# Differential attention of a two-layer trunk: the loads of the next head's queries and keys written in the order of need, and the gates ended at 600 units of attention instead of 640

## The chip, the core and the metric

The kernel runs on one core of one Trainium2 chip. The metric is the device time of one execution in microseconds (us), from the first to the last instruction with the little that lies around them. Lower is better.

## The reference, cut to what matters

Two layers work on 2048 tokens of width 1024. Layer 0 is a windowed attention beside a chunked one, with gates and an output projection; the change leaves it alone. Layer 1 is differential attention with 8 heads: each head has two queries and two keys of 64 columns, and one value of 128 columns.

```
q, k, v, gate = split(h @ w_in)
mask = key chunk <= query chunk                 # chunks of 64 tokens
p1 = softmax(where(mask, q1 @ k1.T / 8, -1e30))
p2 = softmax(where(mask, q2 @ k2.T / 8, -1e30))
o  = (p1 - lam * p2) @ v
o  = rms_norm(o, subln_g) * (1 - lambda_init)
y  = x + (o * silu(gate)) @ w_out
```

All is float32. The kernel keeps each operand as two float32r parts, a high one (H) and a low one (L), and takes a product as two or three matmuls.

## The kernel before, in words

The 2048 tokens are 4 blocks of 512. Layer 1 first projects all tokens (lines named p1) and stores queries, keys and values in DRAM. Then one long stage runs attention, gates and output projection together. It is this stage that the change touches.

**Heads.** The blocks of queries go from 3 down to 0, and in each the 8 heads in order. I write 3.5 for block 3, head 5. A head of block b needs b+1 key tiles for each of its two halves (k0 and k1, with z the number of the key block, so k0z2 is block 2 of the first key) and b+1 value tile pairs. `scores` goes over 4 rows of 128 queries (j); for each it goes over the half m, and for each half over the key blocks z: two matmuls (L867, L868) into a PSUM bank, a maximum on VectorE (L871), an exponential on ScalarE (L874). Then GpSimd scales and combines the two probability rows (L895 to L901). `values` transposes the probabilities (L914), splits them (L917, L918) and multiplies by the values (L921 to L923).

**Side work.** Between these steps stand matmuls that need no attention: `gates` (tiles cG, 288 steps, the eighth chunk of columns of each block of tokens also reloading the 16 tiles of hidden state p1hH, p1hL that the next block of tokens needs), then the output projection of the blocks 3, 2 and 1 (tiles com, 72 steps each), then that of block 0. After the last gates the same 16 tiles take the output weights (wo1H, wo1L). A table, `STAGES1`, says how many side steps shall be done after so many units of attention: a unit is a piece of 128 queries by 128 keys of a head, its scores (both halves) and its values counted half each. A head has 58 units in block 3, 42 in block 2, 26 in block 1 and 10 in block 0, so block 3 ends at 464 units and block 2 at 800.

**Buffers.** A key tile has 4 buffers for each half, as many as one head of block 3 uses. The key tiles of the next head can only be loaded when the last row (j = 3) of the present head has read the old ones, in the order k0z0, k0z1, k0z2, k0z3, k1z0 and on. Queries have 2 buffers, value tiles 4 for each part, gate weights 3 for each part.

**Order.** All transfers are issued by SP, one queue in a fixed order, and an SP row that has to wait holds all rows behind it. Each key tile takes two rows, one for kH and one for kL (L977, L978), queries four for each of qd and ql (L848, L849), values one for each part (L984), gate weights one for each part (L1007). The order on each engine isn't the order of the source: when the program is built, a scheduler places each instruction by its own estimate of when it is ready, and among the ready ones that come first in the source come first. In the source a head began with all its loads: for each key block the keys k0 and k1 and then the value pair (`load`), then the queries inside `scores`.

Of the kernel before, what the change touches and what calls it, by code (L numbers as in the profile page):

```python
# [18 lines left out]
P = 128  # L19
# [12 lines left out]
def f32(ap):  # L32
    return ap.bitcast(F32)
# [52 lines left out]
class Trunk:  # L86
# [727 lines left out]
    def _mix1(self, es):  # L814
# [22 lines left out]

        count = [0]

        def scores(h, b, K, res):  # L840

            tok = slice(b * BLK, (b + 1) * BLK)
            qd = qp.tile([P, 2, BLK], F32R, tag="qd", name=n + "qd")
            ql = qp.tile([P, 2, BLK], F32R, tag="ql", name=n + "ql")
            for m in range(2):
                r = slice(m * HD, (m + 1) * HD)
                for part, q in (("qH", qd), ("qL", ql)):
                    nc.sync.dma_start(f32(q[0:HD, m, :]), s[part][h, r, tok])  # L848
                    nc.sync.dma_start(f32(q[HD:P, m, :]), s[part][h, r, tok])  # L849
            us = res["u"] = []  # L850
            for j in range(NTB):
                t = b * NTB + j
                nk = (t + 1) * P
                cuts = [(c, min(nk, c + 512)) for c in range(0, nk, 512)]
                nb = len(cuts)
                js = slice(j * P, (j + 1) * P)
                nm, la, e = small("nm", 8), small("la", 8), small("e", 8)
                nm, la, e = (x.rearrange("p (m z) -> p m z", m=2) for x in (nm, la, e))
                l, rl = small("l", 2), small("rl", 2)
                rows = []  # L860
                for m in range(2):
                    chunks = []
                    for z, (c, ce) in enumerate(cuts):
                        wd = ce - c
                        ps = pS.tile([P, 512], F32, tag="S", name=n + "S")[:, :wd]
                        kt = K[z][m]
                        mm(ps, qd[:, m, js], kt[:, :wd], start=True, stop=False)  # L867
# [6 lines left out]
                        nc.scalar.activation(chunks[z][:, :wd], ps, AF.Exp, bias=nm[:, m, z:z + 1], accum_out=acc)  # L874
                        yield wd / 256
                    rows.append(chunks)
                if nb > 1:
                    top, pe = small("top", 2), small("pe", 8).rearrange("p (m z) -> p m z", m=2)[:, :, :nb]
                    nc.vector.tensor_reduce(top, nm[:, :, :nb], AX.X, ALU.min)
                    for m in range(2):  # L880
                        nc.scalar.activation(e[:, m, :nb], nm[:, m, :nb], AF.Exp, bias=top[:, m:m + 1], scale=-1.0)
                    nc.vector.tensor_tensor(pe, e[:, :, :nb], la[:, :, :nb], ALU.mult)
                    nc.vector.tensor_reduce(l, pe, AX.X, ALU.add)
                nc.vector.reciprocal(rl, l)  # L884
                cs = small("cs", 8).rearrange("p (m z) -> p m z", m=2)
                if nb > 1:
# [17 lines left out]
        def values(h, b, V, res):  # L904
            us = res["u"]
            O = pO.tile([P, BLK], F32, tag="O", name=n + "O")
            nkt = (b + 1) * NTB
            for kt in range(nkt):
# [8 lines left out]
                nc.scalar.activation(H[:, :wd], tp[:, :wd], AF.Copy)  # L917
                nc.vector.tensor_tensor(L[:, :wd], tp[:, :wd], f32(H[:, :wd]), ALU.subtract)  # L918
                o = O[:, j0 * P:]
                vH, vL = (v[:, kk:kk + P] for v in V[kt // 4])  # L920
                mm(o, vH, H[:, :wd], start=(kt == 0), stop=False, skip_group_check=True)  # L921
                mm(o, vH, L[:, :wd], start=False, stop=False, skip_group_check=True)  # L922
                mm(o, vL, H[:, :wd], start=False, stop=(kt == nkt - 1), skip_group_check=True)  # L923
# [43 lines left out]
            pl, tag = homes[b].pop(0)  # L967
            return pl.tile([P, BLK], F32R, tag=tag, name=n + "y" + tag)

        def load(h, i, K, V):  # L970

            tok = slice(i * BLK, (i + 1) * BLK)
            ks = []
            for m in range(2):
                k = kp.tile([P, BLK], F32R, tag=f"k{m}", name=n + f"k{m}")
                r, o = slice(m * HD, (m + 1) * HD), slice((1 - m) * HD, (2 - m) * HD)
                nc.sync.dma_start(f32(k[r, :]), s["kH"][h, r, tok])  # L977
                nc.sync.dma_start(f32(k[o, :]), s["kL"][h, r, tok])  # L978
                ks.append(k)
            K.append(ks)  # L980
            vs = []
            for part in ("vH", "vL"):
                v = vp.tile([P, BLK], F32R, tag=part, name=n + part)
                nc.sync.dma_start(  # L984
                    f32(v).rearrange("p (t c) -> p t c", t=NTB), s[part][tok, h * P:(h + 1) * P].rearrange("(t p) c -> p t c", p=P)
                )
                vs.append(v)
            V.append(vs)

        room = self.last_hidden  # L990

# [89 lines left out]
        at = [NB - 1]  # L1081

        def heads():
            for b in reversed(range(NB)):
                at[0] = b
                for h in range(8):
                    K, V = [], []
                    for i in range(b + 1):
                        load(h, i, K, V)
                    res = {}  # L1090
                    yield from scores(h, b, K, res)
                    queue.append(values(h, b, V, res))
            queue.append(leave())

        def leave():
# [59 lines left out]
```

## Time and profile before

| | |
|---|---|
| median of 3 runs | 2971.23 us (2970.77 to 2974.16) |
| the profiled execution | 2984.29 us |
| its span, first to last instruction | 2982.5 us |
| mean granted TensorE clock | 0.966 |
| TensorE matmuls busy | 2731.6 us, 92% of the span |
| VectorE, ScalarE, GpSimd busy | 65%, 53%, 54% |
| attention stage of layer 1 | from 1842.7 us to the end |

The profiled execution is 13 us above the median, so a sum made against the one is carried to the other by its ratio. The attention stage is read by stretches between the starts of heads; a start is the first of a head's own L867 matmuls, which are 32 for a head of block 3, 24 in block 2, 16 in block 1 and 8 in block 0, counted in order of time. In these stretches "PEclk" is the granted share of the TensorE clock.

### The profile page before, as it was taken

Reading aid. Unit: us, or ns where it says so; the run is one execution under the profiler, and the core shown is the slowest. Engines: PE = TensorE matmul, PEld = TensorE weight load, DVE = VectorE, ACT = ScalarE, POOL = GpSimd, SP = SyncE. Lnnn points to the kernel's source line nnn. Section 1 sums busy time; section 2 is a strip of 40 time slices with the busy share of each in tenths; the row PEclk is TensorE's granted clock in tenths of the full one; section 3 lists DMA queues with packets and bytes.
Section 4 is the critical chain, followed back from the end, with each engine's and each line's share of the span. In section 5 each row is a group of like instructions: output and inputs, shape, how many; then the busy total and the mean of one; then the engine's idle time right before and its main releaser. Section 6 shows DMA issues by size and latency. Waiting matters only on the chain.

```text
span 2982.5 us, 45078 instructions
## 1 busy us (share of the span) xinstructions
PE 2731.6 (92%) x13672; PEld 2260.0 (76%) x13672; DVE 1927.5 (65%) x4652; ACT 1589.7 (53%) x4135; POOL 1597.2 (54%) x1966
## 2 busy tenths in 40 slices
PE   7999999987888889999999997989989989998889
PEld 5888888876777778777788886767777767776667
DVE  7762475156777775598728852656667876887762
ACT  4443543366666565343344321656667765777661
POOL 3542252145344343267645740767777876888761
PEclk9999999999999999999999999989999999999999
DMA  4673344569988885567884455675767647657683
GB/s 152 224 250 123 103 149 127 185 189 254 258 228 209 221 212 150 185 224 236 264 295 160 127 184 164 192 202 166 217 179 219 193 127 233 170 163 203 164 256 120
DMA packets 422929, 572.40 MB, mean 192 GB/s; under 512 B 47648, under 2 KB 198176, under 8 KB 422688
## 3 DMA queue, kind: packets, MB, share of 16 engines
q1 hardware_dynamic: 422688, 569.53, 65.6%
q8 instruction: 109, 1.79, 0.3%
q14 instruction: 132, 1.08, 0.1%
HBM read 408.95 MB, written 160.43 MB: 191 GB/s over the span
## 4 chain that ended last, share of the span: by engine, by line
PE 66%; DMA 13%; DVE 8%; ACT 3%; issue 2%; POOL 2%; SPq 1%; ACTq 0%; DVEq 0%; POOLq 0%
PE p1mm L214 5%; PE p1mm L215 5%; PE p1mm L216 5%; PE cS L867 3%; PE cS L868 3%; PE ctr L914 3%; PE p0mm L216 3%; PE p0mm L214 3%; PE p0mm L215 3%; PE cO L922 2%; PE com L214 2%; PE com L215 2%; PE com L216 2%; PE cG L214 2%; DMA ck<-kL 2%
## 5 line engine op out<-in xcount | busy, mean ns | idle before, releaser
L874 ACT ACTIVATE cP<-cS,cnm 128x512 f32<-128x512 f32 (+3 forms) x640 | 398.6, 629 | 182.7 <-DVE cnm L871 110.6
L871 DVE TENSOR_REDUCE cnm<-cS 128x1 f32<-128x512 f32 (+3 forms) x640 | 376.5, 602 | 117.3 <-PE cS L868 111.4
L867 PE MATMUL cS<-ck,cqd 128*128 128x512 f32 (+3 forms) x640 | 260.6, 411 | 67.4 <-DMA ck<-kL 24.5
L304 POOL TENSOR_TENSOR p0wL<-p0ws,p0wH 128x512 fp32r<-128x512 f32 (+1 forms) x128 | 155.4, 1246 | 277.1 <-ACT p0wH L303 268.2
L215 PE MATMUL p1mm<-p1wL,p1hH 128*128 128x512 f32 x768 | 302.4, 394 | 0.4 <-POOL p1wL L304 0.4
L214 PE MATMUL p1mm<-p1wH,p1hH 128*128 128x512 f32 x768 | 301.9, 394 | 0.8 <-ACT p1wH L303 0.8
L216 PE MATMUL p1mm<-p1wH,p1hL 128*128 128x512 f32 x768 | 302.1, 394 | 0.0
L901 POOL TENSOR_TENSOR cP<-cP,cP 128x512 f32<-128x512 f32 (+3 forms) x256 | 283.7, 1128 | 1.3
L304 POOL TENSOR_TENSOR p1wL<-p1ws,p1wH 128x512 fp32r<-128x512 f32 x128 | 168.6, 1337 | 138.0 <-ACT p1wH L303 102.3
L214 PE MATMUL p0mm<-p0wH,p0hH 128*128 128x512 f32 (+1 forms) x640 | 237.8, 374 | 3.7 <-ACT p0vt L454 2.8
L215 PE MATMUL p0mm<-p0wL,p0hH 128*128 128x512 f32 (+1 forms) x640 | 238.2, 373 | 0.0
L868 PE MATMUL cS<-ck,cql 128*128 128x512 f32 (+3 forms) x640 | 237.8, 375 | 0.2 <-DMA cql<-qL 0.2
L216 PE MATMUL p0mm<-p0wH,p0hL 128*128 128x512 f32 (+1 forms) x640 | 237.8, 373 | 0.1
L918 DVE TENSOR_TENSOR cptL<-ctr,cptH 128x512 fp32r<-128x512 f32 (+1 forms) x320 | 191.0, 600 | 64.6 <-ACT cptH L917 63.3
L917 ACT ACTIVATE cptH<-ctr 128x512 fp32r<-128x512 f32 (+1 forms) x320 | 170.0, 539 | 92.2 <-PE ctr L914 88.6
L867 PEld LDWEIGHTS cS<-ck,cqd 128*128 128x128 f32 x640 | 124.2, 194 | 108.3 <-ACT cP L874 44.5
L895 POOL TENSOR_SCALAR cP<-cP,ccs 128x512 f32<-128x512 f32 (+3 forms) x288 | 189.2, 674 | 0.0
L914 PE MATMUL ctr<-ident,cP 128*128 128x128 f32 x1088 | 177.8, 280 | 4.5 <-POOL cP L901 2.9
L900 POOL TENSOR_SCALAR cP<-cP,ccs 128x512 f32<-128x512 f32 (+3 forms) x256 | 171.5, 682 | 0.0
L214 PEld LDWEIGHTS p1mm<-p1wH,p1hH 128*128 128x128 f32 x768 | 144.9, 189 | 29.9 <-ACT p1wH L303 1.0
L215 PEld LDWEIGHTS p1mm<-p1wL,p1hH 128*128 128x128 f32 x768 | 145.0, 189 | 29.6 <-POOL p1wL L304 0.8
L887 POOL TENSOR_SCALAR ccs<-ce,crl 128x4 f32<-128x4 f32 (+2 forms) x96 | 27.0, 282 | 261.9 <-DVE crl L884 187.3
(313 smaller groups left out, 7877.8 us busy)
## 6 DMA issues: line engine op xcount, KB each, us to landing
p1ws<-in_od_w_in_dram SPq DMA_DIRECT2D x56, 512.0 KB, 4.7
p0ws<-in_ev_w_in_dram SPq DMA_DIRECT2D x48, 512.0 KB, 4.5
ck<-kH SPq DMA_DIRECT2D x160, 128.0 KB, 3.8
ck<-kL SPq DMA_DIRECT2D x160, 128.0 KB, 4.0
cvH<-vH SPq DMA_DIRECT2D x80, 256.0 KB, 3.7
cvL<-vL SPq DMA_DIRECT2D x80, 256.0 KB, 4.3
cqd<-qH SPq DMA_DIRECT2D x128, 128.0 KB, 4.9
cql<-qL SPq DMA_DIRECT2D x128, 128.0 KB, 4.8
```

Of the source, the lines that this page charges most:

```text
L214: mm(ps, aH, bH, start=first, stop=False)
L215: mm(ps, aH, bL, start=False, stop=False)
L216: mm(ps, aL, bH, start=False, stop=last)
L304: nc.gpsimd.tensor_tensor(l[:, :width], ws[:, k, :width], f32(h[:, :width]), ALU.subtract)
L867: mm(ps, qd[:, m, js], kt[:, :wd], start=True, stop=False)
L868: self.anchor = mm(ps, ql[:, m, js], kt[:, :wd], start=False, stop=True).ins
L871: nc.vector.tensor_reduce(nm[:, m, z:z + 1], ps, AX.X, ALU.max, negate=True)
L874: nc.scalar.activation(chunks[z][:, :wd], ps, AF.Exp, bias=nm[:, m, z:z + 1], accum_out=acc)
L895: nc.gpsimd.tensor_scalar(p1, p1, c1, 1.0, ALU.mult, ALU.mult)
L901: nc.gpsimd.tensor_tensor(p1, p1, p2, ALU.add)
L914: nc.tensor.transpose(tp[:, (j - j0) * P:(j - j0 + 1) * P], us[j][kt // 4][:, kk:kk + P], self.ident)
L918: nc.vector.tensor_tensor(L[:, :wd], tp[:, :wd], f32(H[:, :wd]), ALU.subtract)
```

## The change

Two things are edited. First, the loads are taken apart and moved in the source. The queries of the next head are asked for at row j = 2 of the present one, right after the first exponential there. Each key tile of the next head is asked for at row j = 3, right after the exponential of the scores that read the old tile in its buffer last, so the order in the source is now k0z0 to k0z3 and then k1z0 to k1z3. The values of a head are asked for at row j = 3 of the same head, not ahead of it. Head 3.0 loads its queries and keys before all else. Second, the table has the 288 gate steps done at 600 units instead of 640; the next entry (830 units, 360 steps) stays.

```diff
-    STAGES1 = ((0, 0), (32, 45), (640, 288), (830, 360), (1035, 432), (1088, 490))
+    STAGES1 = ((0, 0), (32, 45), (600, 288), (830, 360), (1035, 432), (1088, 490))
...
-        def scores(h, b, K, res):
+        def load_q(h, b):
...
+            return qd, ql
+
+        def scores(h, b, q, K, res, then):
...
-                        kt = K[z][m]
+                        kt = K[z, m]
...
                         nc.scalar.activation(chunks[z][:, :wd], ps, AF.Exp, bias=nm[:, m, z:z + 1], accum_out=acc)
+                        then(j, m, z)
                         yield wd / 256
...
-        def load(h, i, K, V):
+        def load_k(h, i, m):
...
+            k = kp.tile([P, BLK], F32R, tag=f"k{m}", name=n + f"k{m}")
+            r, o = slice(m * HD, (m + 1) * HD), slice((1 - m) * HD, (2 - m) * HD)
+            nc.sync.dma_start(f32(k[r, :]), s["kH"][h, r, tok])
+            nc.sync.dma_start(f32(k[o, :]), s["kL"][h, r, tok])
+            return k
+
+        def load_v(h, i):
...
-            for b in reversed(range(NB)):
+            order = [(h, b) for b in reversed(range(NB)) for h in range(8)]
+            q, K = load_q(*order[0]), {(i, m): load_k(0, i, m) for m in range(2) for i in range(NB)}
+            for (h, b), nxt in zip(order, order[1:] + [None]):
                 at[0] = b
-                for h in range(8):
-                    K, V = [], []
-                    for i in range(b + 1):
-                        load(h, i, K, V)
-                    res = {}
-                    yield from scores(h, b, K, res)
-                    queue.append(values(h, b, V, res))
+                after, res = [None, {}], {"v": []}
+
+                def then(j, m, z):
+                    if (j, m, z) == (2, 0, 0) and nxt:
+                        after[0] = load_q(*nxt)
+                    if j == NTB - 1:
+                        if nxt and z <= nxt[1]:
+                            after[1][z, m] = load_k(nxt[0], z, m)
+                        if m == 0:
+                            res["v"].append(load_v(h, z))
+
+                yield from scores(h, b, q, K, res, then)
+                queue.append(values(h, b, res))
+                q, K = after
```

What the scheduler makes of it on SP is shown at three places. In the rows ck0 and ck1 are the key halves, cvH and cvL values, cqd and cql queries, cwH and cwL gate weights, p1hH and p1hL the tiles of hidden state; L981 and L982 of the change are L977 and L978 of before, L1013 is L1007, L990 is L984, L1019 and L1020 are L1013 and L1014.

**Place 1, keys of head 3.3.** SP before, from the key tile k0z3 (22991) on; 22964 is k1z0:

```order
L977 DMA ck0_22991<-kH_72 64x512
L977 DMA ck1_22964<-kH_72 64x512
L984 DMA cvH_22314<-vH_74 128x4x128
L984 DMA cvL_22316<-vL_75 128x4x128
L978 DMA ck1_22964<-kL_73 64x512
L977 DMA ck1_22974<-kH_72 64x512
L978 DMA ck1_22974<-kL_73 64x512
L977 DMA ck1_22984<-kH_72 64x512
L978 DMA ck1_22984<-kL_73 64x512
L978 DMA ck0_22991<-kL_73 64x512
```

SP of the change at the same place; k0z3 is 22932, k1z0 is 22945:

```order
L981 DMA ck0_22932<-kH_72 64x512
L982 DMA ck0_22932<-kL_73 64x512
L990 DMA cvH_22918<-vH_74 128x4x128
L990 DMA cvL_22920<-vL_75 128x4x128
L981 DMA ck1_22945<-kH_72 64x512
L982 DMA ck1_22945<-kL_73 64x512
```

The kL half of k0z3 stood nine rows behind its kH half, and now stands right behind it. The heads 3.1, 3.4 and 3.6 had the same nine or so rows between the two halves of k0z3, and head 3.7 seven between those of k0z2; in the change all these pairs are adjacent.

**Place 2, keys of head 3.5.** SP before, from the head's first key row on:

```order
L977 DMA ck0_24279<-kH_72 64x512
L978 DMA ck0_24279<-kL_73 64x512
L977 DMA ck0_24289<-kH_72 64x512
L978 DMA ck0_24289<-kL_73 64x512
L977 DMA ck0_24299<-kH_72 64x512
L978 DMA ck0_24299<-kL_73 64x512
L984 DMA cvH_23644<-vH_74 128x4x128
L984 DMA cvL_23646<-vL_75 128x4x128
```

SP of the change, from the same first key row on:

```order
L981 DMA ck0_24226<-kH_72 64x512
L982 DMA ck0_24226<-kL_73 64x512
L981 DMA ck0_24239<-kH_72 64x512
L982 DMA ck0_24239<-kL_73 64x512
L1019 DMA p1hH_18326<-hH_78 128x512
L1020 DMA p1hL_18327<-hL_79 128x512
L981 DMA ck0_24257<-kH_72 64x512
L982 DMA ck0_24257<-kL_73 64x512
L981 DMA ck0_24271<-kH_72 64x512
L982 DMA ck0_24271<-kL_73 64x512
```

The reload of the hidden tiles, which followed this head's keys before, now falls among them: six of its rows stand between the first and the last of the 16 key rows, which spread over 26 rows instead of 20. At head 2.0 the next reload comes two rows into the keys. At head 3.2 the first reload lay among the keys before and does so still; there the kL half of k0z2 was the 18th row after the first key row and is now the 6th.

**Place 3, the last gate weights, around heads 2.3 to 2.5.** SP before; 28931 and 28941 are the first key tiles of head 2.5:

```order
L1020 DMA g1_76<-cgt_28485 128x512
L977 DMA ck0_28931<-kH_72 64x512
L978 DMA ck0_28931<-kL_73 64x512
L977 DMA ck0_28941<-kH_72 64x512
L984 DMA cvH_28412<-vH_74 128x4x128
L984 DMA cvL_28414<-vL_75 128x4x128
L978 DMA ck0_28941<-kL_73 64x512
L1007 DMA cwH_28511<-wgH_82 128x512
L1007 DMA cwH_28628<-wgH_82 128x512
```

SP of the change; 28192 is the last gate weight tile, 27957 is the last key tile of head 2.3, 28261 holds queries of head 2.4:

```order
L981 DMA ck1_27957<-kH_72 64x512
L982 DMA ck1_27957<-kL_73 64x512
L1013 DMA cwH_28192<-wgH_82 128x512
L1013 DMA cwL_28194<-wgL_83 128x512
L847 DMA cqd_28261<-qH_70 64x512
L848 DMA cqd_28261<-qH_70 64x512
```

Before, the last two gate weight pairs were queued behind keys of head 2.5, which wait for the end of head 2.4. On TensorE head 2.4 then held 5 cG matmuls and no com. In the change the last gate weights follow the keys of head 2.3, and on TensorE the heads 2.3 to 2.7 hold 45, 36, 33, 36 and 36 matmuls of side work. The 16 loads of output weights then stand in one group right ahead of the keys of head 2.4.

More of the change, by code (lines that the diff above doesn't have):

```diff
@@ L849, in scores @@
                     nc.sync.dma_start(f32(q[HD:P, m, :]), s[part][h, r, tok])
+            return qd, ql
+        def scores(h, b, q, K, res, then):
+            qd, ql = q
             us = res["u"] = []
@@ L902, in scores, with values @@
                 us.append(rows[0])
-        def values(h, b, V, res):
+        def values(h, b, res):
             us = res["u"]
@@ L919, in values @@
                 o = O[:, j0 * P:]
-                vH, vL = (v[:, kk:kk + P] for v in V[kt // 4])
+                vH, vL = (v[:, kk:kk + P] for v in res["v"][kt // 4])
                 mm(o, vH, H[:, :wd], start=(kt == 0), stop=False, skip_group_check=True)
@@ L968, in y_tile @@
             return pl.tile([P, BLK], F32R, tag=tag, name=n + "y" + tag)
-        def load(h, i, K, V):
+        def load_k(h, i, m):
             tok = slice(i * BLK, (i + 1) * BLK)
[L973 to L980, printed above, removed]
+            k = kp.tile([P, BLK], F32R, tag=f"k{m}", name=n + f"k{m}")
[4 more added lines that the diff above has]
+        def load_v(h, i):
+            tok = slice(i * BLK, (i + 1) * BLK)
             vs = []
@@ L987, in load @@
                 vs.append(v)
-            V.append(vs)
+            return vs
         room = self.last_hidden
```

## The prediction

> **What bounds the kernel now.** I read the chain of waits first, then the attention stage cut at the ends of the blocks, then who TensorE waits for in it.
>
> ```profile
> span 2982.5 us, 45078 instructions
> ...
> PE 66%; DMA 13%; DVE 8%; ACT 3%; issue 2%; POOL 2%; SPq 1%; ACTq 0%; DVEq 0%; POOLq 0%
> ```
>
> The chain runs through TensorE for two thirds, and the next share is transfers. The windows below are blocks 3, 2, 1 and 0; the columns are the length, the busy time of PE, PEld, DVE, ACT and POOL, the granted clock, and the DMA share.
>
> ```profile
> 1842.70:2266.30 423.60, 385.80 (x1809) 307.99 (x1810) 273.82 (x588) 272.87 (x747) 294.73 (x395) 0.94 0.66 189
> 2266.30:2586.80 320.50, 291.90 (x1396) 230.56 (x1394) 239.61 (x523) 218.29 (x611) 241.26 (x333) 0.95 0.69 193
> 2586.80:2801.40 214.60, 189.33 (x932) 149.77 (x930) 176.67 (x438) 157.98 (x457) 178.88 (x261) 0.96 0.66 178
> 2801.40:2982.50 181.10, 164.57 (x796) 133.50 (x796) 89.34 (x245) 89.09 (x235) 85.55 (x134) 0.98 0.64 187
> ```
>
> TensorE is the fullest engine in every block, and no other is above 84%. So a wait of TensorE that goes away shortens the stage, as long as the other engines follow. In block 2 VectorE needs 239.61 / 8 = 30 us a head, against 320.5 / 8 = 40 us that a head takes. Now TensorE's waits in the stage:
>
> ```profile
> PE cS L867 <- DMA ck<-kL: 24.5, 10, 5.7
> PE cO L922 <- DVE cptL L918: 22.6, 24, 3.8
> PE cS L867 <- ACT cP L874: 22.0, 29, 3.2
> PE cS L867 <- DMA cqd<-qH: 14.2, 2, 12.9
> PE cG L214 <- DMA cwH<-wgH: 11.6, 6, 3.8
> ```
>
> Key loads lead. Where they fall, in TensorE's order of time (the bracket is the idle time before the row and what ended it):
>
> ```profile
> 1842.69 1.72 PE L867 MATMUL cS<-ck,cqd 128*128 128x512 f32 x4 [12.92 <-DMA cqd<-qH]
> ...
> 1946.71 0.77 PE L867 MATMUL cS<-ck,cqd 128*128 128x512 f32 x1 [5.70 <-DMA ck<-kL]
> ...
> 1962.93 0.77 PE L214 MATMUL cG<-p1hH,cwH 128*128 128x512 f32 x1 [3.79 <-DMA cwH<-wgH]
> ...
> 2006.14 0.30 PE L867 MATMUL cS<-ck,cqd 128*128 128x128 f32 x1 [3.54 <-DMA ck<-kL]
> ...
> 2057.90 0.30 PE L867 MATMUL cS<-ck,cqd 128*128 128x128 f32 x1 [0.74 <-DMA ck<-kL]
> ...
> 2110.86 0.30 PE L867 MATMUL cS<-ck,cqd 128*128 128x128 f32 x1 [2.85 <-DMA ck<-kL]
> ...
> 2166.02 0.33 PE L867 MATMUL cS<-ck,cqd 128*128 128x128 f32 x1 [1.55 <-DMA ck<-kL]
> ...
> 2213.89 0.47 PE L867 MATMUL cS<-ck,cqd 128*128 128x512 f32 x1 [1.92 <-ACT cP L874]
> ```
>
> The first is the start of the stage, then come heads 3.2 (two rows), 3.3, 3.4, 3.5, 3.6 and 3.7. The 128-wide ones are the tile k0z3. The last is put down to ScalarE, but it is k0z2 whose kL half was issued late (2209.25 to 2210.48, below), so I count it as a key load.
>
> **The change part by part.** *Keys in order, heads 3.3, 3.4, 3.6, 3.7.* SP around the keys of 3.3, and the late rows of 3.7:
>
> ```profile
> 1995.46 1.09 SPq L977 DMA_DIRECT2D ck<-kH  x2
> ...
> 2000.25 1.23 SPq L978 DMA_DIRECT2D ck<-kL  x2
> ...
> 2205.62 1.20 SPq L977 DMA_DIRECT2D ck<-kH  x2
> ...
> 2209.25 1.23 SPq L978 DMA_DIRECT2D ck<-kL  x2
> ```
>
> At 3.3 kH of k0z3 went out at 1995.46, its kL as the second of the pair at about 2000.9; TensorE got it at 2006.14, after 3.54 us idle, so it was wanted at 2002.6. Right behind its kH the kL goes out at about 1996.0, and with the 5.2 us that this load took (2006.14 - 2000.9) it is there at 2001.2. The wait is gone. At 3.7 the kL half of k0z2 goes out at about 2206.2 instead of 2209.9, 3.7 us earlier for a wait of 1.92. At 3.4 and 3.6 nine rows fall away between the halves, at some 0.6 us each 5 us, for waits of 0.74 and 1.55. So the idle time is 3.54 + 0.74 + 1.55 + 1.92 = 7.75 us. Such a wait also costs clock; at 3.6:
>
> ```profile
> 2164.40:2167.00 2.60, 1.04 (x6) 0.90 (x6) 0.69 (x5) 2.46 (x7) 1.13 (x3) 1.00 0.76 198
> 2167.00:2170.40 3.40, 3.40 (x9) 2.63 (x9) 2.27 (x3) 1.52 (x4) 3.40 (x7) 0.50 1.02 285
> 2170.40:2175.00 4.60, 4.60 (x23) 3.77 (x21) 0.97 (x2) 0.01 (x1) 4.60 (x5) 1.00 0.81 257
> ```
>
> Behind 1.55 us of idle, 3.4 us pass at half clock with TensorE busy all through, which is 1.7 us lost. I count the same for 3.3 and 3.7, and none for the 0.74 us of 3.4: 5.1 us. Together -12.9 us; the bounds are 0, if other rows make the key late again, and -12.9.
>
> The Trainium skill, "TensorE: Matmul & The Clock Gate", section "HAM oscillation — how this bites in real kernels", has the rule that idle gaps above some 3.4 us are what throttles. By it the gaps of 1.55, 1.92 and 2.85 us would cost only themselves, and the sum would come out 5.1 us smaller. The trace disagrees at 3.6, where the gap was 1.55 us and the clock then 0.50.
>
> *Head 3.5.* Its own wait of 2.85 us and 1.7 us of clock go with the old order (-4.5), but now the reload falls among its keys. What such a thing can cost is seen at 3.2; the windows are heads 3.1, 3.2, 3.5 and 2.0:
>
> ```profile
> 1889.20:1936.10 46.90, 45.12 (x228) 37.01 (x227) 32.45 (x73) 31.64 (x88) 32.07 (x44) 1.00 0.74 200
> 1936.10:1998.20 62.10, 51.12 (x229) 40.52 (x228) 34.92 (x77) 35.54 (x96) 40.03 (x54) 0.86 0.72 198
> 2103.20:2160.30 57.10, 50.66 (x242) 39.86 (x242) 36.13 (x79) 36.77 (x101) 40.74 (x55) 0.97 0.78 238
> 2266.30:2309.20 42.90, 39.06 (x187) 30.24 (x185) 27.75 (x65) 27.92 (x77) 29.98 (x41) 0.96 0.96 279
> ```
>
> Head 3.2 took 62.1 us for as many matmuls as 3.1 did in 46.9, so a reload among the keys costs up to 15.2 us; the other end is 0. In the change the first half's keys of 3.5 are through within ten rows, where k0z2 of 3.2 was the 18th, so I take a value near the low end: +4 us at 3.5, +3 us at 2.0.
>
> *Head 3.2.* Its reload stays among the keys, but k0z2 goes out 12 rows earlier. The bytes stay, so part of the 5.70 us turns into a later wait, such as the 3.79 us for gate weights. I take -3, between 0 and -9.1 (5.70 and half of two 3.4 us clock steps).
>
> *Start.* The first query load had ten SP rows ahead of it since the first free value buffer, and now nine; the gate weights come ahead of it instead of behind:
>
> ```profile
> 1829.84 0.37 SPq L984 DMA_DIRECT2D cvH<-vH  x1
> ...
> 1836.58 0.84 SPq L848 DMA_DIRECT2D cqd<-qH  x1
> ```
>
> 6.7 us for ten rows is 0.7 a row: -1 us of the 12.92, between -2 and +1. The values move behind; head 3.0's aren't used before its scores end.
>
> *Gates at 600.* At 464 units there were 45 + 243 x 432/608 = 218 steps done, and there will be 45 + 243 x 432/568 = 230. Twelve steps of three matmuls, 0.2 us each (23 in 4.60 us above), move 7 us from block 2 to block 3. TensorE is 91% busy in both (385.80 / 423.60, 291.90 / 320.50), so that is zero as work. What counts is where side work is missing. The windows are heads 2.2, 2.3, 2.4 and 2.5; then cG alone, in 2.3 and in the stretch after 2.4's start:
>
> ```profile
> 2342.70:2380.70 38.00, 37.04 (x191) 29.70 (x189) 29.83 (x69) 28.22 (x81) 35.70 (x47) 1.00 0.65 184
> 2380.70:2417.60 36.90, 33.98 (x163) 26.66 (x160) 27.36 (x62) 26.44 (x75) 22.92 (x34) 0.95 0.58 157
> 2417.60:2461.50 43.90, 32.75 (x143) 24.06 (x142) 34.77 (x67) 28.64 (x81) 35.55 (x50) 0.87 0.48 121
> 2461.50:2511.90 50.40, 48.27 (x234) 39.04 (x233) 28.58 (x69) 28.99 (x80) 24.00 (x34) 0.94 0.73 217
> ```
>
> ```profile
> 2380.70:2417.60 36.90, 12.15 (x45) 9.07 (x45) 1.20 (x2) 0.95 0.58 157
> 2418.90:2458.30 39.40, 0.07 (x1) 0.00 (x0) 0.62 (x1) 0.90 0.41 104
> ```
>
> For 39 us TensorE had no gate work, since the last weights stood behind the keys of 2.5; it waited on the chain of scores, at a clock of 0.87. In head 2.5 all of it came at once:
>
> ```profile
> 2449.39 0.45 SPq L977 DMA_DIRECT2D ck<-kH  x1
> ...
> 2452.91 1.05 SPq L1007 DMA_DIRECT2D cwH<-wgH  x2
> ```
>
> Evenly filled, the two heads should take what 2.2 and 2.3 take: 43.9 + 50.4 = 94.3 against 38.0 + 36.9 = 74.9, so 19.4 us. The output weights must still come, now at 2.3 and 2.4; a reload next to a head cost 42.9 - 38.0 = 4.9 us (2.0 against 2.2). I take -15, between 0 and -19.4.
>
> *The other moves* (queries asked for at j = 2, values at j = 3, keys in blocks 1 and 0) I cost at nothing: they wait for the same buffers, and each has a head's length of cover; without it a late load costs some 1.5 to 3 us, as the waits above.
>
> Sum: -12.9 - 4.5 + 7 - 3 - 1 - 15 = -29.4 us on 2984.3, which is 0.990; of the median 2971.23 that makes **2942 us**. What can be told from no change is about 0.2%, 6 us.
>
> **Rivals.** (a) *Short stalls don't lower the clock.* If the half clock behind waits below 3 us has another cause, the 1.7 us at 3.5, 3.6 and 3.7 don't come back: -24.3, 2947 us. Against it stands the clock row of 3.6. This is what the rule of the Trainium skill above would give.
> (b) *The order of the keys is moot.* The scheduler ordered the ready loads already, and keys come free too late whatever the order: the terms for keys and 3.2 are zero, 3.5 keeps its stall. Left are +7 - 1 - 15 = -9, so 2962. For it speaks that the keys were loaded within a few us of need everywhere; against it the nine rows between two halves of one tile.
> (c) *Block 2 evens out wholly.* Heads 2.3 to 2.7 each come 2.6 us nearer to VectorE's 30 than the 36.9 of 2.3, 13 us, and 3.2 loses its whole 9.1, 6 more than counted: 2923. For it speaks the even side work, 33 to 45 matmuls a head; against it that 2.3, as even, took 36.9.
> (d) *No change.* The gap in side work isn't what made 2.4 slow, VectorE with 34.77 us busy is: then the term of -15 is zero, and the output weights ahead of 2.4's keys cost up to the 15.2 of 3.2: 2972.
> (e) *Slower: loads in front of keys.* Reloads now stand among or right ahead of the keys of 3.5, 2.0 and 2.4. At 15.2 us each that is 45.6, where the sum has 7 and 4.4: +34, and 3.2 gains nothing: 2979. It outweighs the gains from 13 us a head on, and can be told from 14.6 on. The 62.1 of 3.2 speaks for it, the short stretches of rows against it.
>
> **How the numbers follow.** My forecast has 0.46, with its own range of 2930 to 2957; (a) 0.08, (b) 0.16, (c) 0.12, (d) 0.09, (e) 0.09. Faster is the first four, 0.82; same 0.09; slower 0.09. The range of 8 in 10 takes in the forecast, (a), (b) and (c): 2914 to 2968.
>
> **What would show it.** Key waits of L867's successor below some 12 us instead of 24.5; heads 3.3, 3.4, 3.6, 3.7 each 1 to 6 us shorter for the same matmuls; 2.4 and 2.5 near 37 us each; 3.5 and 2.0 no longer than 57 and 46. I am wrong if heads 3.5 or 2.4 take over 60 and 45 us, or if the key waits go but heads keep their length, VectorE or ScalarE then ending TensorE's waits.

## The result and the profile after

| | before | after |
|---|---|---|
| median | 2972.69 us (2970.77 to 2977.65, 4 runs) | 2944.16 us (2932.18 to 2951.29, 4 runs) |
| profiled execution | 2984.29 | 2947.06 |
| ratio, 95% interval | | 0.9897 [0.9861, 0.9934] |

The change makes the kernel about 1.0% faster, 28.5 us between the medians; the forecast was 2942, in a range of 2914 to 2968.

The page of the profile after: the span, and the chain of waits.

```profile
span 2945.3 us, 45089 instructions
...
PE 64%; DMA 14%; DVE 12%; ACT 4%; POOL 3%; issue 2%; SPq 1%; DVEq 0%; ACTq 0%; POOLq 0%
```

The chain still runs through TensorE. Blocks 3, 2, 1 and 0 after, in the columns of the windows shown before:

```profile
1846.10:2250.40 404.30, 381.76 (x1834) 303.40 (x1835) 270.19 (x588) 272.77 (x747) 295.12 (x393) 0.97 0.73 211
2250.40:2551.90 301.50, 278.79 (x1374) 224.34 (x1372) 243.54 (x523) 215.16 (x608) 241.21 (x331) 0.97 0.69 190
2551.90:2761.00 209.10, 186.60 (x923) 148.55 (x921) 176.88 (x438) 157.77 (x459) 181.71 (x265) 0.96 0.67 180
2761.00:2945.20 184.20, 170.58 (x802) 136.96 (x802) 87.18 (x246) 89.49 (x236) 87.13 (x134) 0.95 0.66 186
```

Blocks 3 and 2 are 19 us shorter each; blocks 1 and 0 together changed by 2 us. A stretch can be split in three: the idle time of TensorE (length less busy time), the time lost to the clock (length times one less PEclk), and the work at full clock that is left. For block 3 that was 37.8 + 23.9 + 361.9 us and is now 22.5 + 10.1 + 371.6; for block 2 it was 28.6 + 17.1 + 274.8 and is 22.7 + 10.2 + 268.6 (the clock from the unrounded record). So work moved from block 2 to block 3, and idle time and clock were won in both. TensorE's waits in the kernel after (total, count, longest):

```profile
PE cS L872 <- DMA ck<-kL: 20.5, 15, 3.4
PE cO L928 <- DVE cptL L924: 17.8, 17, 3.4
PE cS L872 <- ACT cP L879: 17.6, 33, 2.0
PE cS L872 <- DMA cqd<-qH: 12.2, 1, 12.2
```

Key waits lead as before, with 20.5 us against 24.5 (in a second profile of each kernel, taken below, 21.6 against 20.7, so as a sum they did not fall). But they are in other places. The windows are heads 3.2 to 3.7 and 2.0, then 2.4 to 2.6:

```profile
1937.00:1991.60 54.60, 48.78 (x229) 37.38 (x227) 35.50 (x78) 35.03 (x96) 35.99 (x47) 0.94 0.75 216
1991.60:2042.20 50.60, 48.54 (x242) 38.66 (x241) 36.17 (x76) 35.85 (x97) 42.90 (x59) 1.00 0.59 175
2042.20:2095.30 53.10, 50.30 (x249) 39.86 (x249) 37.77 (x81) 37.45 (x102) 42.32 (x56) 1.00 0.79 225
2095.30:2153.80 58.50, 51.43 (x244) 41.00 (x243) 35.50 (x77) 36.27 (x99) 37.92 (x51) 0.91 0.69 196
2153.80:2200.50 46.70, 45.03 (x229) 36.08 (x227) 34.31 (x77) 34.51 (x96) 35.61 (x47) 1.00 0.62 182
2200.50:2250.40 49.90, 49.12 (x244) 38.79 (x243) 35.33 (x79) 36.04 (x99) 42.85 (x58) 1.00 0.91 256
2250.40:2295.20 44.80, 40.28 (x196) 32.23 (x194) 29.44 (x66) 28.11 (x78) 32.58 (x46) 0.96 0.71 196
```

```profile
2405.00:2439.00 34.00, 31.47 (x158) 24.92 (x159) 27.50 (x63) 25.22 (x71) 28.16 (x39) 1.00 0.62 164
2439.00:2473.20 34.20, 31.34 (x163) 25.46 (x162) 27.82 (x66) 25.32 (x75) 28.29 (x39) 1.00 0.62 167
2473.20:2514.30 41.10, 36.26 (x166) 28.99 (x166) 30.83 (x64) 26.88 (x76) 29.47 (x42) 0.88 0.78 213
```

Heads 3.3, 3.4, 3.6 and 3.7 run at a clock of 1.00 with 1 to 3 us idle: no key wait above 0.3 us is left in them. The waits now sit at the heads with a reload. TensorE, heads 3.2 (first row) and 3.5:

```profile
1946.08 0.76 PE L872 MATMUL cS<-ck,cqd 128*128 128x512 f32 x1 [2.92 <-DMA ck<-kL]
...
2098.99 0.47 PE L872 MATMUL cS<-ck,cqd 128*128 128x512 f32 x1 [1.97 <-DMA ck<-kL]
...
2104.41 0.77 PE L872 MATMUL cS<-ck,cqd 128*128 128x512 f32 x1 [3.38 <-DMA ck<-kL]
...
2108.41 0.76 PE L872 MATMUL cS<-ck,cqd 128*128 128x512 f32 x1 [0.97 <-DMA ck<-kL]
```

And why at 3.5; SP in the kernel after, the rows that go out just ahead of the tile waited for:

```profile
2095.02 0.59 SPq L982 DMA_DIRECT2D ck<-kL  x1
2095.70 0.54 SPq L1019 DMA_DIRECT2D p1hH<-hH  x1
2096.33 0.38 SPq L990 DMA_DIRECT2D cvH<-vH  x1
2096.82 0.45 SPq L990 DMA_DIRECT2D cvL<-vL  x1
2097.83 0.33 SPq L1020 DMA_DIRECT2D p1hL<-hL  x1
2098.34 0.45 SPq L981 DMA_DIRECT2D ck<-kH  x1
```

Between two key tiles stand a reload pair and a value pair, and p1hL starts 0.56 us after the row ahead of it is done (2096.82 + 0.45 = 2097.27): SP is waiting there, with the keys behind it. So the next key is held back by 2.7 us (2095.61 to 2098.34), of which the four rows themselves take 1.7; in the kernel before most key rows of this head went out some 0.6 us apart. The 16 key rows of 3.5 are spread over 20.7 us, against 14.4 before. SP's own waits from the first of them to the last, after and then before (total, count, longest), one row of each:

```profile
SPq L981 <- DMA p1hL<-hL: 1.3, 2, 0.8
```

```profile
SPq L977 <- PE cS L868: 2.5, 2, 1.3
```

After there are 21 such waits, 10.8 us together, and 12 of them, 5.9 us, end when a transfer lands; before there are 5, 4.1 us together, and none of them ends so. The transfers are slower as well. From the issue of a key row of this head to its landing it took, after and then before:

```profile
DMA to landing us min/median/max: 3.8/5.3/7.1
```

```profile
DMA to landing us min/median/max: 2.7/3.5/6.0
```

So the keys go out later and each takes longer; the first wait above (1.97 us) is for k0z2, the other two for k1z0 and k1z2, keys of the second half.

### The profile page after: what moved, and what is told of

Read it like the earlier page. It is cut to its first block, busy times and chain, and to the rows that moved or that the text cites. A ratio compares the mean times of both kernels' runs of the same rounds, so it can differ in the third digit from the quotient of the medians.

```text
span 2945.3 us, 45089 instructions
## 1 busy us (share of the span) xinstructions
PE 2719.2 (92%) x13672; PEld 2253.5 (77%) x13672; DVE 1923.4 (65%) x4652; ACT 1588.8 (54%) x4135; POOL 1601.1 (54%) x1966
## 4 chain that ended last, share of the span: by engine, by line
PE 64%; DMA 14%; DVE 12%; ACT 4%; POOL 3%; issue 2%; SPq 1%; DVEq 0%; ACTq 0%; POOLq 0%
PE p1mm L216 4%; PE p1mm L215 4%; PE p1mm L214 4%; PE p0mm L214 3%; PE p0mm L215 3%; PE p0mm L216 3%; PE cS L872 3%; PE cS L873 3%; PE ctr L920 3%; DVE cnm L876 2%; DMA mks<-bkL 2%; PE cO L928 2%; PE mom L214 2%; PE cG L214 2%; PE mom L215 2%
## 5 line engine op out<-in xcount | busy, mean ns | idle before, releaser
L872 PE MATMUL cS<-ck,cqd 128*128 128x512 f32 (+3 forms) x640 | 262.9, 415 | 56.9 <-DMA ck<-kL 20.5
L216 PEld LDWEIGHTS p1mm<-p1wH,p1hL 128*128 128x128 f32 x768 | 145.2, 189 | 29.0
```

The source lines that it names most:

```text
L216: mm(ps, aL, bH, start=False, stop=last)
```

## The experiments

**The change again.** The kernel after, unchanged, for a second profile and more runs.

> The changed kernel once more, beside the others of this group, so that they can be compared with it on one chip. Both theories: 2944 us, between 2932 and 2951 as in its first four runs, ratio to before 0.987 to 0.993.

Measured: 2946.81 us (2933.86 to 2952.16, 7 runs) against 2971.57 for before, ratio 0.9913 [0.9879, 0.9947]. The two profiles of the kernel after agree by head to about 2 us in blocks 3 and 2, except for 2.4 (34.0 and 39.5 us) and 2.6 (41.0 and 36.6). So a difference of one head below some 5 us can't be read from one profile in block 2.

**Before again.** The kernel before, for a second profile of it.

> The kernel of before once more, for a second profile of it: how much do the lengths of single heads scatter between two executions? Expected: block 3 within 8 us of 423.6, heads 2.4 and 2.5 together within 6 us of 94.3, the waits for k0z3 of 3.3 to 3.6 again 0.5 to 4 us each. If the gain of block 3 (19.3 us) or of 2.4 and 2.5 (26 us) were scatter of one execution, one of them would be missed by this second profile.

Measured: 2979.47 us. Its heads 3.2, 3.5, 2.4 and 2.5:

```profile
1940.90:2000.60 59.70, 49.88 (x228) 39.67 (x228) 34.30 (x77) 35.59 (x96) 40.09 (x54) 0.91 0.69 203
2104.40:2161.30 56.90, 51.28 (x243) 39.66 (x243) 36.29 (x79) 36.68 (x101) 40.76 (x55) 0.97 0.77 238
2414.90:2459.60 44.70, 32.76 (x144) 24.18 (x143) 34.82 (x67) 28.61 (x81) 35.85 (x50) 0.87 0.46 118
2459.60:2509.30 49.70, 47.77 (x234) 38.83 (x233) 28.52 (x69) 28.90 (x81) 23.80 (x33) 0.95 0.73 219
```

The same places are slow, by the same amounts within 3 us. But block 3 as a whole takes 415.4 us, 8.2 less than in the first profile and just outside what was expected; against it the second profile of after, with 402.5, is 13 us shorter and not 19. And the start of the stage lies at 1848.5 us, 5.8 later than in the first profile, 4.8 of it in work ahead of the stage that the change doesn't touch. Below, terms are means over both profiles of each kernel.

**Loads alone.** The change with the old table.

```diff
-    STAGES1 = ((0, 0), (32, 45), (600, 288), (830, 360), (1035, 432), (1088, 490))
+    STAGES1 = ((0, 0), (32, 45), (640, 288), (830, 360), (1035, 432), (1088, 490))
```

> The loads of the changed kernel with the table of before (gates end at 640 units). Theory of two causes (keys in the order of need gain in block 3, the even side work gains in block 2): block 3 is 12 to 20 us shorter than the 423.6 us of before, heads 2.4 and 2.5 still take about 90 us together, total 2953 to 2961 us. Rival, all from the table: 2971 us, block 3 as before. Rival, all from the loads: 2944 us.

Measured: 2960.19 us (12 runs), ratio 0.9969 [0.9948, 0.9991]. Blocks 3 and 2:

```profile
1840.00:2242.00 402.00, 379.48 (x1809) 300.52 (x1810) 271.19 (x588) 272.85 (x747) 295.75 (x395) 0.97 0.69 200
2242.00:2559.40 317.40, 289.65 (x1389) 229.50 (x1387) 240.54 (x523) 219.04 (x609) 243.99 (x333) 0.95 0.67 194
```

Block 3 loses 35.0 us to idle time and clock, against 32.6 and 29.7 after and 61.7 and 49.9 in the two profiles of before: block 3's gain comes from the loads. Block 2 loses 43.1, against 45.7 and 45.2 before, so it gains next to nothing; its heads 2.4 and 2.5 take 45.0 and 43.5 us. This is what the theory of two causes expected.

**Table alone.** The kernel before with gates ended at 600.

```diff
-    STAGES1 = ((0, 0), (32, 45), (640, 288), (830, 360), (1035, 432), (1088, 490))
+    STAGES1 = ((0, 0), (32, 45), (600, 288), (830, 360), (1035, 432), (1088, 490))
```

> The kernel of before with gates ended at 600 units, loads as before. Theory of two causes: heads 2.4 and 2.5 take 68 to 75 us together instead of 94.3, the waits for keys of heads 3.3, 3.4 and 3.6 stay (0.7 to 3.5 us each, there are nine rows between the halves of k0z3 as before), head 3.5 has the reload among its keys and takes 57 to 62 us; total 2953 to 2963 us. Rival, all from the table: 2944 us. Rival, all from the loads: 2971 us.

Measured: 2958.69 us (12 runs), ratio 0.9956 [0.9933, 0.9978]. Heads 2.4 and 2.5 take 75.8 us, just above the 68 to 75 expected, and lose 13.8 us instead of 22, but others lose more: a key wait of 8.18 us at 3.5, one of 5.56 at 2.0, one of 7.08 at 2.6. In this profile block 3 loses 51.4 us and block 2 46.1, as much as before. In the kernel after it loses 32.9 and 32.5. So in these profiles each part alone leaves block 2 as it was, and together they take 13 us out of it. My reading, which no run tests by itself, is that the table brings the loads of the side work in front of keys, and that with the keys in order this costs less. In the times the two parts (0.31% and 0.44%) add up to 0.75%, against 1.03% and 0.87% for both; the intervals are too wide to show the joint part there.

**Reloads set between the keys of two heads.** Points are added to the table so that the gate chunk that reloads ends elsewhere in a head.

```diff
-    STAGES1 = ((0, 0), (32, 45), (600, 288), (830, 360), (1035, 432), (1088, 490))
+    STAGES1 = ((0, 0), (32, 45), (111, 72), (285, 144), (458, 216), (600, 288), (830, 360), (1035, 432), (1088, 490))
```

> The changed kernel with a table of more points, (111, 72), (285, 144), (458, 216), (600, 288): the reloads of the hidden tiles then stand between two heads' keys, with 2, 0 and 0 of their rows among the keys of heads 3.2, 3.5 and 2.0 instead of 6, 6 and 0 to 4. Theory (a reload among the keys costs the head some 5 to 10 us): 3.2, 3.5 and 2.0 together fall from 157.8 us to 140 to 148, total 2928 to 2936 us. Rival, the transfers cost the same wherever they stand, since the same bytes have to come: 2944 us as the changed kernel, the wait moves to the gate weights.

Measured: 2932.19 us (6 runs), ratio 0.9876 [0.9842, 0.9910]. Block 3:

```profile
1840.80:2230.70 389.90, 375.56 (x1808) 296.65 (x1809) 267.59 (x588) 272.90 (x747) 296.67 (x394) 0.99 0.70 207
```

Of the reload rows two stand among the keys of 3.2 and none among those of 3.5, where there were six and six. Head 3.5 loses 4.9 us instead of 12.2 and 9.1, head 3.2 2.9 instead of 9.2 and 8.5, and block 3 in all 19.1 instead of 32.6 and 29.7. Head 2.0 has no reload row among its keys any more and loses as much as in the kernel after (6.0), so the three heads take 151.5 us and not the 140 to 148 expected. The time is as expected, and reloads among the keys of 3.2 and 3.5 are a real cost of the changed kernel.

**No reloads, after and before.** The loads of the hidden tiles between blocks of tokens are left out.

```diff
-                        if c == 7 and b:
-                            before = slice((b - 1) * BLK, b * BLK)
-                            nc.sync.dma_start(f32(hH), s["hH"][k, :, before])
-                            nc.sync.dma_start(f32(hL), s["hL"][k, :, before])
-                        elif c == 7:
+                        if c == 7 and not b:
```

> The changed kernel without the three reloads of the hidden tiles (48 loads of 256 KB; the gates of blocks 2 to 0 then use the hidden tiles of block 3, so that their values are others). Theory (a reload among the keys is what costs 3.2, 3.5 and 2.0): these three fall from 157.8 us to 135 to 145 and the others stay, total 2924 to 2934 us, no better than the kernel with the reloads off the keys by more than 8 us. Rival (the transfers as such hold the stage up, wherever they stand): all of block 3 falls, total below 2915 us.

> The kernel before without the reloads of the hidden tiles between blocks of tokens (the gates of the later blocks then use the wrong hidden state; the 16 output weight loads stay). The same cut took the changed kernel from 54.5 to 47.7 us at head 3.2, from 58.5 to 48.7 at 3.5 and from 44.8 to 40.5 at 2.0, 21 us together. Theory A (the forecast's terms of +4 at 3.5 and +3 at 2.0: the change moved a cost onto the keys that was not there before): the kernel before gains at 3.2 alone, 62.1 to some 47, and 3.5 and 2.0 lose at most 3 us each; time of before less 15 to 18 us, about 2953. Theory B (a reload costs the same wherever its rows stand, so the change added nothing): 3.5 and 2.0 fall by about 10 and 4 us as they did in the changed kernel, time of before less 26 us or more, about 2943.

Measured: from the kernel after 2918.74 us (5 runs), ratio to before 0.9836 [0.9815, 0.9856]; from the kernel before 2958.89 us (12 runs), ratio 0.9956 [0.9937, 0.9975]. Heads 3.2, 3.5 and 2.0, first with the change, then without it:

```profile
1932.60:1980.30 47.70, 45.89 (x228) 35.44 (x227) 35.56 (x78) 34.72 (x96) 36.01 (x47) 1.00 0.67 191
2083.30:2132.00 48.70, 47.90 (x244) 38.63 (x242) 35.44 (x77) 35.90 (x99) 37.89 (x51) 1.00 0.67 195
2227.10:2267.60 40.50, 39.38 (x196) 31.13 (x194) 31.19 (x66) 27.79 (x79) 32.58 (x46) 1.00 0.70 203
```

```profile
1940.20:1988.80 48.60, 45.71 (x229) 36.31 (x229) 34.75 (x77) 35.29 (x96) 40.12 (x54) 1.00 0.63 181
2094.00:2149.30 55.30, 51.26 (x245) 40.11 (x244) 38.67 (x81) 36.81 (x102) 42.80 (x58) 0.97 0.56 170
2251.40:2288.10 36.70, 35.60 (x180) 28.84 (x179) 26.63 (x63) 27.18 (x76) 29.96 (x39) 1.00 0.74 211
```

With the reloads gone the three heads of the changed kernel take 136.9 us, as expected; the time of 2918.74 lies between the two theories, under the 2924 to 2934 of the one and above the 2915 of the other. The key rows of 3.5 there take 3.7 us from issue to landing in the median, against 5.3 with the reloads.

In idle time and clock (one profile of each kernel without reloads) a reload costs, before: 14.3 us at 3.2 (17.2 as the mean of two profiles, less 2.9), 2.0 at 3.5 and 3.9 at 2.0. With the change: 7.0, 9.9 and 5.2. That is 20 us before and 22 after: the change moved the cost from 3.2 to 3.5 and hardly changed its sum. Theory A is right for 3.5, theory B for 2.0. The spans of the profiled executions agree with the heads: without reloads they are 22.7 us shorter before and 20.3 after. The medians say something else: 11.4 us won before, less than either theory had, and some 26 after (2944.16 or 2946.81 less 2918.74). The profiles don't explain this difference, and with runs of one kernel 10 to 25 us apart it stays open.

**A hole in the side work.** Points are added so that side work stops in head 2.4 and is done in 2.5, as before, while the gates and their weights stay where the change has them.

```diff
-    STAGES1 = ((0, 0), (32, 45), (600, 288), (830, 360), (1035, 432), (1088, 490))
+    STAGES1 = ((0, 0), (32, 45), (600, 288), (606, 290), (650, 290), (690, 316), (830, 360), (1035, 432), (1088, 490))
```

> The changed kernel with the points (606, 290), (650, 290), (690, 316) put in the table: head 2.4 then holds 6 matmuls of side work and 2.5 holds 69 (36 and 33 in the changed kernel, 5 and 79 before); output weights and keys stand as in the changed kernel. Theory (the missing side work made 2.4 and 2.5 slow): both together go from 68 to 74 us back to 82 to 94, total 2955 to 2965 us. Rival (VectorE or the late keys of 2.5, not the missing side work): both together stay below 78 us, total 2944 us.

Measured: 2939.36 us (6 runs), ratio 0.9909 [0.9879, 0.9939], the same as with the change. Heads 2.4 and 2.5, all work, then tile com alone:

```profile
2395.60:2431.10 35.50, 29.08 (x133) 20.99 (x134) 29.10 (x62) 24.93 (x72) 28.49 (x38) 0.95 0.57 151
2431.10:2470.20 39.10, 39.01 (x201) 32.06 (x199) 32.39 (x67) 27.64 (x76) 31.23 (x45) 1.00 0.48 142
```

```profile
2395.60:2431.10 35.50, 1.70 (x6) 1.13 (x6) 0.00 (x0) 0.95 0.57 151
2431.10:2470.20 39.10, 18.24 (x69) 12.58 (x69) 2.06 (x3) 1.00 0.48 142
```

The hole is there, 6 side matmuls in 2.4 and 69 in 2.5, against 5 and 79 before. Head 2.4 does wait, 6.4 us idle; but 2.5 then waits for nothing (39.01 us busy of 39.10). The pair loses 9.8 us with the clock and the stall at the border, against 6.3 and 11.1 in the kernel after and 22 before. A hole in the side work alone is not what made 2.4 and 2.5 slow. What the kernel before had in 2.4 besides, in its second profile; first two waits of TensorE, then two rows of VectorE ahead of the first of them:

```profile
2443.12 0.50 PE L922 MATMUL cO<-cptL,cvH 128*128 128x512 f32 x1 [3.78 <-DVE cptL L918]
...
2456.51 0.79 PE L214 MATMUL cG<-p1hH,cwH 128*128 128x512 f32 x1 [3.98 <-DMA cwH<-wgH]
```

```profile
2437.37 5.09 DVE L882 TENSOR_TENSOR cpe<-ce,cla 128x6 f32<-128x6 f32 x1
2442.39 0.68 DVE L918 TENSOR_TENSOR cptL<-ctr,cptH 128x512 fp32r<-128x512 f32 x1
```

The gate matmul stands in TensorE's order whether its weights are there or not, and everything behind it waits. The two stalls are 7.8 of the 11.9 us idle in 2.4, and 11.9 us at half clock come on top. The stall on the split is VectorE's: the split (L918) that TensorE wanted stood behind a product of 128x6 elements that took 5.09 us, and in the kernel after the slowest of the same operation in 2.4 is this:

```profile
2435.22 0.47 DVE L888 TENSOR_TENSOR cpe<-ce,cla 128x6 f32<-128x6 f32 x1
```

The four of them in 2.4 take 8.5 us before (first profile) and 0.9 after, which is all of the difference in VectorE's busy time there (34.77 and 27.50 us). Why they are so slow isn't shown. In the kernel with the loads alone, too, the weights come late (a wait for cwL of 2.36 us), the split is waited for (3.52 us), and the pair loses 18.0. All four profiles with gates up to 640 have both stalls in 2.4, a VectorE busy for 34.8 to 36.3 us there, and 15.6 to 17.9 us lost in that head; the nine others have 26.0 to 33.6 us and lose 0.1 to 9.6. So late weights and a slow VectorE come together in these runs, and no run took one of them away alone: which of the two made 2.4 slow stays open.

**Keys alone ahead.** The queries and values of a head are asked for at its own start, keys as in the change.

```diff
-                after, res = [None, {}], {"v": []}
+                after, res = {}, {"v": [load_v(h, i) for i in range(b + 1)]}
+                q = load_q(h, b)
...
-                    if (j, m, z) == (2, 0, 0) and nxt:
-                        after[0] = load_q(*nxt)
-                    if j == NTB - 1:
-                        if nxt and z <= nxt[1]:
-                            after[1][z, m] = load_k(nxt[0], z, m)
-                        if m == 0:
-                            res["v"].append(load_v(h, z))
+                    if j == NTB - 1 and nxt and z <= nxt[1]:
+                        after[z, m] = load_k(nxt[0], z, m)
...
```

> The changed kernel with only the keys asked for ahead: queries and values are asked for at the start of their own head, as before. Theory (queries and values gain nothing by their move): 2944 us, 2936 to 2952, as the changed kernel. Rival (the queries asked for ahead, or the values that no longer stand among the next head's keys, bring part of it): 2950 to 2960 us.

Measured: 2936.92 us (6 runs), ratio 0.9890 [0.9871, 0.9909]. That is as much as the whole change gives, and block 3 loses 33.4 us to idle time and clock, about as after. The gain of the loads is that of the keys; the move of queries and values is worth nothing that these runs can tell.

**Both in one.** Keys alone ahead, with the table points that set the reloads between heads.

> The two versions that came out ahead of the changed kernel in one: only the keys are asked for ahead, queries and values at the start of their own head, and table points that set the reloads of the hidden tiles between the keys of two heads. Theory A (the costs are separate: taking the reloads out of the keys gave some 13 us on the changed kernel, the queries and values give nothing): 2920 to 2930, head 3.5 near 52 us and the idle time with its half clock in block 3 near 19 us, as against 33. Theory B (the lower time of the keys-only version had the same source as that of the moved reloads): no lower than 2932.

Measured: 2919.59 us (2917.06 to 2931.79, 6 runs), ratio 0.9830 [0.9806, 0.9854], the fastest version with no load left out, and well ahead of both kernels. Blocks 3 and 2 (the profiled execution, 2931.79 us, is the slowest of the six):

```profile
1848.70:2240.90 392.20, 374.01 (x1809) 294.07 (x1810) 269.87 (x588) 271.93 (x747) 295.51 (x395) 1.00 0.69 205
2240.90:2538.70 297.80, 280.08 (x1399) 223.30 (x1397) 238.86 (x522) 215.57 (x607) 240.22 (x328) 0.99 0.76 209
```

Block 3 loses 20.1 us (18.2 idle, 1.9 of clock) and head 3.5 takes 50.6 us: theory A. It is ahead of the moved reloads alone (0.9876 [0.9842, 0.9910]) by more than was expected of queries and values, but the intervals overlap.

**Output weights off the keys.** The changed kernel with points that also move the output projection.

```diff
-    STAGES1 = ((0, 0), (32, 45), (600, 288), (830, 360), (1035, 432), (1088, 490))
+    STAGES1 = ((0, 0), (32, 45), (111, 72), (285, 144), (458, 216), (590, 288), (700, 315), (830, 360), (1035, 432), (1088, 490))
```

> The changed kernel with the reloads set between the keys of two heads and the output weights, too, moved off the keys: none stands among the keys of head 2.6 any more (four rows did). Theory A (the forecast's 4.4 us for output weights next to a head is paid at 2.4 and at 2.6): 3 to 6 us less than with the reloads moved alone, 2926 to 2929, head 2.6 near 36 us instead of 42. Theory B (the output weights were hidden behind side work): the same 2932 within 0.2%.

Measured: 2932.22 us (6 runs), ratio 0.9866 [0.9842, 0.9889], against 2932.19 with the reloads moved alone: theory B. Head 2.6 went from 42.0 to 38.6 us, and the time did not follow. What the output weights cost next to a head is too small to see.

## Why the prediction was right, term by term

The terms against idle time and lost clock of TensorE, in us, in the two profiles of each kernel. A stall is counted with the head whose matmul stands behind it:

| term | forecast | before | after | change of the means |
|---|---|---|---|---|
| wait at the start of the stage | -1 | 12.9, 13.9 | 12.2, 11.3 | -1.7 |
| heads 3.3, 3.4, 3.6, 3.7 | -12.9 | 25.6, 19.6 | 7.4, 6.7 | -15.5 |
| head 3.2 | -3 | 19.5, 14.9 | 9.2, 8.5 | -8.4 |
| head 3.5 | -4.5 + 4 | 8.1, 7.3 | 12.2, 9.1 | +3.0 |
| head 2.0 | +3 | 5.5, 4.5 | 6.2, 6.0 | +1.1 |
| heads 2.4 and 2.5 | -15 | 21.8, 22.3 | 6.3, 11.1 | -13.4 |
| all else in the stage | 0 | 76.9, 76.2 | 74.0, 77.3 | -0.9 |
| sum | -29.4 | 170.3, 158.7 | 127.5, 130.0 | -35.8 |

The spans of these profiles differ by 33.1 us in the mean (2980.1 and 2947.0), the medians by 28.5 and 24.8. Both profiles of before are 11 to 13 us above the median of the runs taken with them, those of after 3 to 4, so the table is somewhat too large as a whole, and so was the sum of the forecast, which was read in one of them. The change and its size were forecast rightly, but that 2942 lies 2 us off the first median is luck: the terms are off by up to 5 us each and partly cancel, and the two medians of after differ by 2.7.

**Right: keys in order.** The four heads lost their key waits, and with them the clock: 10.2 and 5.1 us of clock loss before, 0 after. The term came to -15.5, beyond the bound of -12.9. Loads alone give block 3 its gain, and keys alone give all of it. Rival (b) falls.

**Mis-sized: the reloads.** I put 3.2 at -3 and the collision at +4 and +3. It was -8.4, +3.0 for the whole of 3.5 (by the runs without reloads a collision of +7.9 there, 9.9 less 2.0) and about +1. The step that failed was to read the price off a count of rows for the first half of the keys: "the first half's keys of 3.5 are through within ten rows". They were, and still k0z2 was waited for (1.97 us); but the longest wait, 3.38 us, was for k1z0, in the second half, which the count left out. Behind it stand SP's waits (10.8 us from first to last key row, against 4.1) and slower transfers (5.3 us in the median, against 3.5). Taking the reload rows out from among the keys took both away with the cost (5.3 us of waits, 3.9 us in the median, 4.9 us lost at 3.5), so how much each of the two counts is not shown. In 3.2 the full 9.1 of its upper bound nearly came back, as rival (c) had it. The other half of (c) did not come: heads 2.3 to 2.7 took 34 to 41 us each, where it had some 34. Together the three heads gave -4.3 where -0.5 was forecast.

**Right in size, wrong in cause: block 2.** The pair 2.4 and 2.5 came to 68.2 us (first profile) from 94.3, where -15 was taken. But 9.6 of these 26 us are work that went to other heads (at full clock 72.5 us before, 62.9 after), so 16.5 were won in this profile (15.5 in the table, which counts the 0.9 us stall at the start of 2.4 as well), and 13.4 in the mean of both. "What counts is where side work is missing" is refuted by the kernel with the hole. Rival (d) was right that the hole isn't the cause, and wrong that the term is zero. Whether VectorE is the cause, as (d) had it, is not settled: its 34.77 us in 2.4 became 27.50, a stall of 3.8 us went with them, and so did the late weights. The 4.4 us for output weights were not seen.

**Right: moved gate steps cost nothing.** 7 us of work were to move from block 2 to block 3. In the means block 2 has 5.2 us less work at full clock, block 3 8.5 more.

**Wrong: the key waits.** They were to fall below 12 us and stand at 20.5 (21.6 in the second profile), no lower than the 20.7 of before's second profile: those at 3.5 and 2.0 that the change made, and small ones in block 2, took the place of the old. Head 3.5 was to take no more than 57 us and took 58.5 and 56.4. Also 3.4 did not get shorter (50.2 and 50.0 us before, 53.1 and 52.6 after): it holds six more microseconds of work, and lost 2.8 us instead of 6.8.

**Rival (a), the clock.** 1.7 us each were counted for stalls of 1.55 to 3.54 us, from one row behind the shortest. A table-only run has the same stall at the same place, followed by full clock (the stall of head 3.6, and the 3.4 us behind it):

```profile
2164.05 0.30 PE L867 MATMUL cS<-ck,cqd 128*128 128x128 f32 x1 [1.55 <-DMA ck<-kL]
```

```profile
2164.00:2167.40 3.40, 3.35 (x16) 2.81 (x17) 1.73 (x5) 2.06 (x7) 2.52 (x5) 1.00 1.01 291
```

So a single stall of that length may or may not cost clock. The clock of these heads came back because such stalls went away in number. The time itself, 2944 to 2947, can't tell 2942 from the 2947 of (a).

**Rival (e).** Reloads in front of keys did cost 8 us at 3.5 where they are new, not 15.2, and 3.2 gained, so the sign was not in danger. But the position of the reloads was worth another 11 to 15 us, and 20 to 27 together with queries and values left alone (by the ratios and by the medians).

## What to carry to other kernels

On a queue that issues in order, write a load where its buffer comes free and in the order in which it is read, and then look at what else stands between: a row that has to wait holds every load behind it, wherever its bytes go, and a load that goes out beside others can take longer to land. Before a slow stretch is put down to missing work, split its length into idle time, clock and work at full clock, since work that only moves looks like a gain. And profile each side twice: one head differed by 5 us between two profiles of one kernel.

## What the runs showed of the hardware

How often a stall brings half clock grows with its length. Over the stage in the 13 profiles, stalls of TensorE that did not begin at half clock, and how many had a stretch of half clock begin between the stall's own start and 3.5 us after its end:

| idle, us | stalls | with half clock |
|---|---|---|
| 0.4 to 1.2 | 393 | 40 |
| 1.2 to 1.6 | 71 | 15 |
| 1.6 to 2.0 | 57 | 28 |
| 2.0 to 3.0 | 88 | 68 |
| above 3.0 | 69 | 69 |

The Trainium skill, "TensorE: Matmul & The Clock Gate", section "HAM oscillation — how this bites in real kernels", gives idle gaps above some 3.4 us as the rule. The runs agree in that all 69 stalls above 3 us bring half clock (47 of them while the stall still lasts; 13 are the waits at the start of the stage), and differ below: from 2 to 3 us it is three in four, so these can't be counted as free.

TensorE's work ahead of the stage, which no edit here touches, ended between 1823.4 and 1835.5 us in these profiles. That is 0.4% of the span from one execution to the next, more than some of the effects looked for.
